# One chunk of the later modulation with each of the first five chunks of a block of w_out, in place of one with every second

## Chip, core and metric

The kernel runs on one core of one Trainium2 chip. TensorE multiplies matrices, VectorE and ScalarE (ACT) do the elementwise work, GpSimd (POOL) and SyncE (SP) issue transfers. The metric is the device time of one execution in microseconds; the number compared is the median of several executions.

## The reference

One inference step of one trunk layer over 384 tokens, 128 of context and 256 latent ones, of width 2048, all in 32-bit floats. Cut to what matters here:

```python
shift1, scale1, gate1, shift2, scale2, gate2 = split(silu(c) @ w_mod + b_mod, 6)   # c, and c_ctx for the context
h = rmsnorm(x, norm1) * (1 + scale1) + shift1
q_a, k_a, v_a, o_a, g, q_b, k_b, v_b, gate_a, gate_b = split_columns(h @ w_in)
y_a = bidirectional mLSTM of the a parts;  y_b = differential attention of the b parts
y = sigmoid(gate_a) * (y_a @ w_pa) + sigmoid(gate_b) * (y_b @ w_pb)
x = x + gate1 * (y @ w_out)
h = rmsnorm(x, norm2) * (1 + scale2) + shift2
u = depthwise convolution of width 3 over tokens of (h @ w_up)
x = x + gate2 * ((silu(u_a) * u_b) @ w_down)
result: rmsnorm(x, final_norm), and the caches and states of the context
```

`w_mod` is 2048 x 12288, that is 24 column blocks of 512; block 4 s + i belongs to the s-th of the six vectors. `shift1` and `scale1` (blocks 0 to 7) are needed before the first projection. The rest is the later modulation: gate1 (8 to 11), shift2 (12 to 15), scale2 (16 to 19), gate2 (20 to 23).

## The kernel before

All weights come from HBM in chunks of 512 KB, one `Chunk` each: SP loads it into one of six buffers (`raw`), and a chunk for a matmul is split there, in two halves (`PARTS`), into a high and a low half-precision part: ACT writes `hi` (L361), VectorE writes `lo` = raw - hi (L362); `hi` and `lo` have five buffers each. A product takes three matmuls, hi*hi, hi*lo and lo*hi: L371 to L373 where the weights are the stationary operand (`add_wstat`), L428 to L430 where the tokens are (`add_xstat`).

The order of the work is a list, `chunks`, written by hand: matmul chunks, chunks without a split, and calls (`mark`). `run()` walks it: at each place it issues the loads of up to five chunks ahead, splits up to two halves ahead, and calls `due()` before each half, which runs small work that `defer(n, f)` has put off by n halves. A scheduler below fixes the order of instructions on each engine, and gives out buffers. `settle` runs all that is still put off.

The later modulation is done on VectorE, not by matmuls. The list `by_dve` holds its 128 chunks, eight for each block, in this order: blocks 8, 16, 12; 9, 17, 13; 10, 18, 14; 11, 19, 15 (groups 0 to 3); then 20, 21, 22, 23 (group 4). Each chunk (`late_mod`, L263 and L265) has two slices of `w_mod` that are multiplied by a scalar per partition and added to an accumulator, `lacc`, once for each of two conditions: four instructions of 128 x 512. There is one buffer for the accumulator. After a block's eighth chunk, `late_sum` adds the accumulator over partitions on TensorE (L292), ACT copies the result, and either `late_out` transposes it (L301) into the modulation table, or, for the two gates, `late_row` adds the bias and writes it as a row to DRAM, by eight small transfers of POOL, from where a chunk `add_rows` reads it back over all partitions.

`spread(main, share)` mixes: it appends the chunks of `main` and, after each, as often as the running sum of `share` reaches one, the next chunk of `by_dve`. The stages in order:

- `phase_vb`, `phase_a`, `phase_gb`, `phase_ga` (parts of `w_in`, `w_pb`, `w_pa`): 16, 33, 48 and 48 chunks, shares `dens[0]` to `dens[3]`;
- four blocks of w_out, 512 columns each, `phase_out(b)`: eight matmul chunks, each 18 matmuls of 128 x 512, with the row of gate1 ahead of the last. `settle`, then the first five chunks with share `dens[4]`, then `finish_late(b)`, which puts whatever is left of groups up to b into the list, `settle`, and the other chunks. At a block's end VectorE multiplies by the gate and adds to x (L924, L926), TensorE transposes the result (L948), and ACT and VectorE scale it into the input of w_up (L953, L954, L957);
- eleven groups g of w_up, `add_up(g)`, 16 chunks each, share `dens[5]`; after g = 2 comes `finish_late(4)` and a `settle`, after g = 2, 4, 6, 8 and 10 a quarter or so of the products with w_down (`add_down`, `keep`);
- the last tokens, the norm and the outputs.

```python
for b in range(4):
    mark(settle)
    main = taken(phase_out, b)
    spread(main[:5], dens[4])
    finish_late(b)
    mark(settle)
    chunks.extend(main[5:])
...
for g in range(ngr):
    spread(taken(add_up, g), dens[5])
    if g == 2:
        finish_late(4)
        mark(settle)
```

Of the kernel before, what the change touches and what calls it, by code (L numbers as in the profile page):

```python
# [35 lines left out]
def hybrid_step(  # L36
# [1161 lines left out]
            chunks.append(by_dve.pop(0)[1])  # L1198


    dens = (.25, .25, .75, .8, .5, .5)

    def settle():
        while later:
# [130 lines left out]
```

## Time and profile before

| | |
|---|---|
| median of 3 runs | 2313.24 us |
| lowest and highest | 2309.41 and 2313.98 us |
| the profiled execution | 2311.3 us |
| its span, first to last instruction | 2309.6 us |
| mean granted clock of TensorE | 0.993 |
| read from HBM | 381.18 MB, 167 GB/s over the span |

The profile is one execution. Times in it count from the start of its span. A busy time of TensorE is that of overlapping matmuls: one of 128 x 512 lasts 0.40 us and the next starts 0.23 us after it. In a stretch row, each engine has its busy time and, in brackets, its instructions; then come the granted clock of TensorE as a share of full speed, the mean busy share of the 16 DMA engines, and GB/s. In a row of the timeline stand start and duration, engine, line, operation, operands, and in square brackets the idle time before it with what ended it. PEld is TensorE's loading of stationary operands, which runs beside the matmuls. A name before `<-` is written, those behind it are read.

### The profile page before, as it was taken

To read this page: it belongs to the slowest core of one execution; us is meant where nothing else is said; L and a number is where in the kernel's file an instruction comes from. 1 tells how busy PE (TensorE), PEld (TensorE's weight loads), DVE (VectorE), ACT (ScalarE), POOL (GpSimd) and SP (SyncE) were. 2 spreads that over 40 slices of the span, in tenths; PEclk is the share of its full clock that TensorE was granted. 3 is DMA by queue.
4 is the path that set the end of the run, shared out by engine and by line. 5 is a ranking of instruction groups with operands and counts; after the bars stand their busy time and mean duration, and the time that the engine had idled before them with its cause. 6 is when DMAs were issued, how large, how long until landed. Compare 5 with 4: busy or idle time off the path is not lost.

```text
span 2309.6 us, 34978 instructions
## 1 busy us (share of the span) xinstructions
PE 2245.2 (97%) x12814; PEld 2065.4 (89%) x12814; DVE 1637.9 (71%) x3413; ACT 1015.9 (44%) x2104; POOL 146.5 (6%) x261
## 2 busy tenths in 40 slices
PE   6999999999999999999999959999999999999998
PEld 5888997889999999987899958998899899989987
DVE  5777877777889989876789875565555555556576
ACT  5322355575555433333455522454344345434541
POOL 1000222211111100010000000000000000000000
PEclk9999999999999999999999979999999999999999
DMA  8787654445566677775656545444543543453462
GB/s 269 252 247 240 182 140 126 128 130 147 171 175 176 181 217 235 208 255 157 191 181 188 179 149 161 129 127 131 152 128 120 155 137 119 136 155 120 137 209 84
DMA packets 300300, 388.22 MB, mean 168 GB/s; under 512 B 17669, under 2 KB 215829, under 8 KB 300129
## 3 DMA queue, kind: packets, MB, share of 16 engines
q1 hardware_dynamic: 293552, 377.34, 53.6%
q0 software_dynamic: 5712, 7.09, 1.1%
q8 instruction: 100, 1.64, 0.3%
q10 hardware_dynamic: 864, 1.57, 0.2%
q14 instruction: 72, 0.58, 0.1%
HBM read 381.18 MB, written 4.76 MB: 167 GB/s over the span
## 4 chain that ended last, share of the span: by engine, by line
PE 89%; DVE 4%; DMA 3%; ACT 1%; issue 1%; POOL 0%; SPq 0%; DVEq 0%; ACTq 0%; POOLq 0%
PE mm L371 20%; PE mm L372 20%; PE mm L373 20%; PE mm L428 7%; PE mm L429 7%; PE mm L430 7%; DMA raw<-in_w_mod_dram 2%; DVE lacc L265 1%; PE mb L227 1%; DVE lo L362 1%; PE mm L1066 1%; PE mm L1065 1%; PE mm L1064 1%; PE sd L829 0%; DMA raw<-in_w_in_dram 0%
## 5 line engine op out<-in xcount | busy, mean ns | idle before, releaser
L361 ACT CAST hi<-raw 128x512 fp32r<-128x512 f32 x960 | 591.0, 620 | 1012.4 <-PE mm L372 526.4
L362 DVE TENSOR_TENSOR lo<-raw,hi 128x512 fp32r<-128x512 f32 x960 | 659.7, 693 | 482.3 <-ACT hi L361 478.3
L371 PE MATMUL mm<-hh,hi 128*128 128x386 f32 x1408 | 479.4, 340 | 0.0
L372 PE MATMUL mm<-hl,hi 128*128 128x386 f32 x1408 | 479.0, 340 | 0.0
L373 PE MATMUL mm<-hh,lo 128*128 128x386 f32 x1408 | 478.2, 340 | 0.0
L265 DVE SCALAR_TENSOR_TENSOR lacc<-raw,scT,lacc 128x512 f32<-128x512 f32 x480 | 342.0, 747 | 23.0 <-DMA raw<-in_w_mod_dram 22.8
L371 PE MATMUL mm<-xg,hi 128*128 128x384 f32 x1024 | 354.4, 347 | 2.2 <-ACT hi L361 1.4
L373 PE MATMUL mm<-xg,lo 128*128 128x384 f32 x1024 | 345.5, 337 | 0.0
L372 PE MATMUL mm<-xl,hi 128*128 128x384 f32 x1024 | 345.3, 337 | 0.0
L371 PEld LDWEIGHTS mm<-hh,hi 128*128 128x128 f32 x1408 | 267.7, 190 | 0.9 <-ACT hi L361 0.4
L372 PEld LDWEIGHTS mm<-hl,hi 128*128 128x128 f32 x1408 | 267.0, 190 | 0.2
L373 PEld LDWEIGHTS mm<-hh,lo 128*128 128x128 f32 x1408 | 266.6, 189 | 0.0
L371 PEld LDWEIGHTS mm<-xg,hi 128*128 128x128 f32 x1024 | 192.4, 188 | 21.9 <-issue 12.3
L428 PE MATMUL mm<-hi,gh 128*128 128x512 f32 x480 | 188.1, 398 | 15.3 <-ACT hi L361 14.8
L373 PEld LDWEIGHTS mm<-xg,lo 128*128 128x128 f32 x1024 | 192.2, 188 | 1.0 <-issue 0.8
L429 PE MATMUL mm<-lo,gh 128*128 128x512 f32 x480 | 190.5, 397 | 2.5 <-DVE lo L362 2.5
L372 PEld LDWEIGHTS mm<-xl,hi 128*128 128x128 f32 x1024 | 192.5, 188 | 0.5 <-issue 0.4
L430 PE MATMUL mm<-hi,gl 128*128 128x512 f32 x480 | 189.8, 395 | 0.0
L428 PEld LDWEIGHTS mm<-hi,gh 128*128 128x128 f32 x480 | 90.7, 189 | 37.1 <-ACT hi L361 15.0
L429 PEld LDWEIGHTS mm<-lo,gh 128*128 128x128 f32 x480 | 90.8, 189 | 23.8 <-DVE lo L362 3.0
L430 PEld LDWEIGHTS mm<-hi,gl 128*128 128x128 f32 x480 | 90.8, 189 | 21.5
L506 DVE TENSOR_TENSOR qk<-qk,mm 128x384 f32<-128x384 f32 x160 | 86.0, 549 | 25.0 <-PE mm L373 24.7
(333 smaller groups left out, 2974.0 us busy)
## 6 DMA issues: line engine op xcount, KB each, us to landing
raw<-in_w_mod_dram SPq DMA_DIRECT2D x192, 512.0 KB, 4.3
raw<-in_w_up_dram SPq DMA_DIRECT2D x176, 512.0 KB, 3.5
raw<-in_w_in_dram SPq DMA_DIRECT2D x160, 512.0 KB, 4.5
raw<-in_w_down_dram SPq DMA_DIRECT2D x80, 512.0 KB, 3.9
raw<-in_w_out_dram SPq DMA_DIRECT2D x32, 512.0 KB, 4.3
raw<-gate SPq DMA_DIRECT2D x28, 512.0 KB, 4.3
raw<-in_w_pb_dram SPq DMA_DIRECT2D x16, 512.0 KB, 3.8
raw<-in_w_pa_dram SPq DMA_DIRECT2D x16, 512.0 KB, 4.4
```

Of the source, the lines that this page charges most:

```text
L227: T.matmul(self.bank[32 * q:32 * q + 32, 0:self.width], lhsT=scT[:, k, 2 - 2 * i:34 - 2 * i], rhs=w[:, kk], start=i == 0 and k < 4, stop=i ...
L265: V.scalar_tensor_tensor(acc[:, j], w[:, kk], col, acc[:, j], ALU.mult, ALU.add)
L361: A.copy(h, v)
L362: V.tensor_tensor(l, v, h.bitcast(F32), ALU.subtract)
L371: T.matmul(ps, lhsT=wh, rhs=xh, start=first, stop=False)
L372: T.matmul(ps, lhsT=wh, rhs=xl, start=False, stop=False)
L373: T.matmul(ps, lhsT=wl, rhs=xh, start=False, stop=last)
L428: T.matmul(ps, lhsT=xh_[:, ts_], rhs=h[:, kk], start=k == ks[0], stop=False)
L429: T.matmul(ps, lhsT=xh_[:, ts_], rhs=l[:, kk], start=False, stop=False)
L430: T.matmul(ps, lhsT=xl_[:, ts_], rhs=h[:, kk], start=False, stop=k == ks[-1])
L506: V.tensor_tensor(dst[h][:, :NTOK], dst[h][:, :NTOK], ps, ALU.add)
L1064: T.matmul(ps, lhsT=gh[:, ts_], rhs=h, start=k == KL[0], stop=False)
```

## The change

The fifth of the six shares, used for the first five chunks of each block of w_out, goes from .5 to 1. With .5, `spread` appends a late chunk after the second and the fourth of the five; with 1, after each. Which late chunks are left for `finish_late` and for the groups of w_up follows from it; no line else is changed.

```diff
-    dens = (.25, .25, .75, .8, .5, .5)
+    dens = (.25, .25, .75, .8, 1, .5)
```

## The prediction

> **What bounds the kernel now.** I read the page's engine shares and its 40 slices first, then busy times by stretch, then the instructions in order of time where a slice falls off, and last the stage that the change loads.
>
> ```profile
> span 2309.6 us, 34978 instructions
> PE 2245.2 (97%) x12814; PEld 2065.4 (89%) x12814; DVE 1637.9 (71%) x3413; ACT 1015.9 (44%) x2104; POOL 146.5 (6%) x261
> PE   6999999999999999999999959999999999999998
> PEclk9999999999999999999999979999999999999999
> ```
>
> TensorE is busy 97% of the span, so only what leaves it idle can be won, 64.4 us in all (2309.6 - 2245.2). One slice in the middle, the 24th (each is 57.7 us, so 1328 to 1386 us), falls to 5 tenths, and there alone the granted clock falls too. The stretches around it:
>
> ```profile
> core 0: us, PE busy (x) PEld busy (x) DVE busy (x) ACT busy (x) POOL busy (x), PEclk, DMA share, GB/s
> 900.00:1000.00 100.00, 100.00 (x597) 99.07 (x596) 87.26 (x145) 37.63 (x76) 10.77 (x21) 1.00 0.77 236
> 1002.00:1037.00 35.00, 34.67 (x164) 27.47 (x163) 25.06 (x45) 11.04 (x19) 0.00 (x0) 1.00 0.68 220
> 1037.00:1073.00 36.00, 35.83 (x161) 28.64 (x160) 23.12 (x44) 13.14 (x25) 0.00 (x0) 1.00 0.52 161
> 1073.00:1109.00 36.00, 35.66 (x160) 28.43 (x159) 23.26 (x44) 12.94 (x25) 0.00 (x0) 1.00 0.55 163
> 1109.00:1144.00 35.00, 34.76 (x170) 27.43 (x169) 26.27 (x51) 14.07 (x32) 0.00 (x0) 1.00 0.60 194
> 1180.00:1352.00 172.00, 172.00 (x992) 171.11 (x991) 141.45 (x273) 82.97 (x158) 8.38 (x18) 1.00 0.58 178
> 1352.00:1386.00 34.00, 10.13 (x55) 6.90 (x54) 31.03 (x56) 7.98 (x16) 4.01 (x8) 0.60 0.50 147
> 1386.00:1500.00 114.00, 114.00 (x559) 101.82 (x558) 60.38 (x103) 40.38 (x70) 0.00 (x0) 1.00 0.47 146
> 1500.00:1700.00 200.00, 200.00 (x1038) 187.25 (x1038) 114.23 (x214) 86.14 (x159) 0.00 (x0) 1.00 0.44 135
> 1700.00:1900.00 200.00, 200.00 (x1039) 187.25 (x1038) 114.94 (x215) 86.20 (x159) 0.00 (x0) 1.00 0.44 135
> 1900.00:2100.00 200.00, 200.00 (x1039) 187.22 (x1038) 113.54 (x213) 85.45 (x157) 0.00 (x0) 1.00 0.44 136
> ```
>
> The rows at 1002, 1037, 1073 and 1109 are the four blocks of w_out, one each. From 1180 to 1352 the w_up groups g = 0 to 2 run with TensorE full; from 1386 to 2100 it is full again. Between them, in 34 us, it is busy 10.13 us, while VectorE is busy 31.03. What VectorE does there:
>
> ```profile
> 1327.89 34.02 SPq L345 DMA_DIRECT2D raw<-in_w_mod_dram  x9
> 1352.96 0.34 PE L373 MATMUL mm<-hh,lo 128*128 128x386 f32 x1
> 1353.22 0.66 PE L292 MATMUL sd<-lacc,ones 128*32 128x128 f32 x16
> 1357.46 4.72 DVE L265 SCALAR_TENSOR_TENSOR lacc<-raw,scT,lacc 128x512 f32<-128x512 f32 x7
> 1361.44 15.98 DVE L265 SCALAR_TENSOR_TENSOR lacc<-raw,scT,lacc 128x512 f32<-128x512 f32 x24
> 1364.20 5.67 SPq L345 DMA_DIRECT2D raw<-in_w_down_dram  x3
> 1367.98 1.14 ACT L361 CAST hi<-raw 128x512 fp32r<-128x512 f32 x2 [11.88 <-DMA raw<-in_w_down_dram]
> 1368.65 1.65 PE L428 MATMUL mm<-hi,gh 128*128 128x512 f32 x3 [14.76 <-ACT hi L361]
> 1376.90 1.67 PE L292 MATMUL sd<-lacc,ones 128*32 128x128 f32 x16 [6.60 <-DVE lacc L265]
> 1381.08 0.80 PE L429 MATMUL mm<-lo,gh 128*128 128x512 f32 x1 [2.50 <-DVE lo L362]
> 1381.67 0.63 PE L430 MATMUL mm<-hi,gl 128*128 128x512 f32 x1
> 1382.10 0.63 PE L429 MATMUL mm<-lo,gh 128*128 128x512 f32 x1
> 1385.51 0.42 PE L429 MATMUL mm<-lo,gh 128*128 128x512 f32 x1
> 1385.77 0.40 PE L430 MATMUL mm<-hi,gl 128*128 128x512 f32 x1
> 1386.00 0.39 PE L428 MATMUL mm<-hi,gh 128*128 128x512 f32 x1
> ```
>
> This is block 23 of the later modulation: eight chunks (`finish_late(4)` at the end of g = 2) in a row with no matmul chunk between them. SP issues their loads one behind the other, the w_down loads stand behind them in the queue and get a buffer only at 1364; VectorE works through the eight chunks from 1357 to 1377; the low halves (L362) of the first w_down chunk come behind them, and TensorE waits for ACT's high half, for the accumulator, then for the low half.
>
> **The change part by part.** First a count by the list that `spread` draws from. It holds 128 late chunks. The shares .25, .25, .75 and .8 over 16, 33, 48 and 48 matmul chunks take 4, 8, 36 and 38 of them, so 86 are gone when w_out begins. Before: two in each block of w_out and two more by `finish_late(3)` make 10; the groups g = 0 to 2 take 8 each, and 32 - 24 = 8 are left for the row above. After: five per block make 20; 22 are left; g = 0 and 1 take 8 each, g = 2 takes 6 with its second to twelfth chunk, and `finish_late(4)` finds none. So ten late chunks move into w_out, and the eight in a row are gone. Work is neither added nor removed.
>
> 1. What the eight in a row cost TensorE. The last matmul of w_up starts at 1352.96, the first one at full spacing at 1385.51: 32.55 us. Needed work in it: that last matmul (0.18), three L428 at the 0.23 us of the rows at 1385.77 and 1386.00 (0.7), the matmuls that ran between 1381.08 and 1385.51 (ten, at 0.23: 2.3) and two sums of an accumulator (L292, 0.66 each by the undisturbed one: 1.3). Together 4.5, so 28.0 us are lost. It agrees with the stretch row: 34.00 - 10.13 = 23.9 us idle, and some 4 us in which TensorE counts as busy at half pace.
>
> 2. What remains at that place. The queue of w_down chunks then follows w_up chunks directly. Of such boundaries there are three more later (after g = 4, 6 and 8), and in the rows from 1386 to 2100 TensorE is full, so I cost the boundary at nothing. Its cover is that `add_down(0)` reads products of g = 0 and 1 only, and that its loads are no longer behind eight others.
>
> 3. VectorE in w_out. A late chunk is four instructions of L265 (the first of a block has two of L263), and 24 of them took 15.98 us in the row above: 0.666 each, 2.66 us a chunk. Blocks 0, 1 and 2 get three more, 8.0 us; block 3 one more than the four it has now, 2.7 us. What VectorE has to spare in block 1:
>
> ```profile
> L362 DVE TENSOR_TENSOR lo<-raw,hi 128x512 fp32r<-128x512 f32 x17 | 11.6, 688 | 10.1 <-ACT hi L361 10.1
> L265 DVE SCALAR_TENSOR_TENSOR lacc<-raw,scT,lacc 128x512 f32<-128x512 f32 x8 | 5.7, 748 | 2.6 <-DMA raw<-in_w_mod_dram 2.6
> ```
>
> These are the groups of VectorE from 1037 to 1073. It waits 10.1 us for ACT's high halves and 2.6 for late loads, 12.7 of 36 us. Less 8.0 this leaves 4.7, so the block as a whole holds the work. Block 3 shows it nearly: it has four late chunks today, VectorE is busy 26.27 of 35, and TensorE loses 0.24 us. The stage ahead of w_out is another measure: there the share is .8, VectorE is busy 87.26 of 100 and TensorE 100.00. With 1 to 1, the splits of a chunk (two L362) and a late chunk are some 1.2 + 2.7 = 3.9 us against 18 matmuls of 0.23, 4.2 us: 93%. Tight is only the start of blocks 1 to 3, where the evacuation of the block before (three L924, three L926) and its rescaled rows (L954, L957) come on top, about 7 us. VectorE then runs behind by some 2 to 3 us and catches up in chunks six to eight, which carry no late chunk. Five buffers each of `hi` and `lo` are five half chunks of 2.1 us, so a lag of that size should not reach TensorE.
>
> 4. Loads. First the waits of VectorE from 1000 to 1160 us (total, times, longest), two short stretches with the fullest DMA engines, and the page's line on the late loads (median us to landing):
>
> ```profile
> DVE lacc L265 <- DMA raw<-in_w_mod_dram: 6.3, 6, 1.7
> DVE lacc L263 <- PE sd L292: 2.8, 2, 1.4
> 990.00:1010.00 20.00, 19.67 (x102) 17.96 (x101) 17.81 (x30) 7.70 (x15) 4.34 (x9) 1.00 0.99 353
> 1000.00:1002.00 2.00, 2.00 (x13) 2.00 (x12) 2.00 (x4) 1.15 (x2) 0.00 (x0) 1.00 1.04 387
> raw<-in_w_mod_dram SPq DMA_DIRECT2D x192, 512.0 KB, 4.3
> ```
>
> Three more loads of 512 KB in the five chunks of a block (24.5 us of its 36) are 64 GB/s over that stretch. Even on top of the fullest of these blocks' means (220) that is under the 353 to 387 GB/s that shorter stretches here reach, and block 1 with its 161 comes to about the 236 that the stage ahead carries at a full TensorE. In SP's queue the ten loads now stand between w_out loads instead of w_up and w_down loads; six buffers are shared one to one, so a w_out load gets its buffer later. VectorE runs in order. A late load lands 1.05 us after VectorE wants it (6.3 over 6 waits), at most 1.7. Behind the waiting L265 stand the low halves, and TensorE waits for those. Five waits a block of 1.05 are 5.3 us against the 4.7 spare: 0.6 us over. Bounds: with no wait nothing; with the worst, 1.7, 8.5 - 4.7 = 3.8 us a block, 15 in four. Below nothing at most the 1.1 us that TensorE idles in the four block rows now (0.33 + 0.17 + 0.34 + 0.24). I take 1.5 us for all four, near the mean wait, because in the stage at .8 TensorE loses nothing.
>
> 5. Sums that move. Block 15's sum, transposes and scale rows come in w_out's block 1 rather than 3; block 20's sum, bias row and gate row (on POOL a fill, four small loads, four small stores) in block 3 rather than in w_up, where POOL shows 0.00 busy in that row; those of 21 to 23 inside w_up. There is one accumulator, so block 21's first chunk (fourth of block 3) waits for block 20's sum on TensorE: once, 1.4 us by the row of L263 above. It is inside the 1.5.
>
> Sum against the profiled execution (2311.3 us, span 2309.6): 2311.3 - 28.0 + 1.5 = 2284.8. That execution lies 1.9 us under the median of the three runs (2313.24), inside their spread of 4.6, so I forecast 2285 us.
>
> One rule weighed against a row: the stretch with the stall has a granted clock of 0.60 where its neighbours have 1.00, and matmuls come every 0.43 us (1381.67, 1382.10) for 4.4 us after the stall, which costs 2.1 us of the 28.0. The Trainium skill, in "TensorE: Matmul & The Clock Gate", section "What's actually happening", says that an idle window of about 3.4 us halves the clock and as long a busy one restores it. By that figure the slow tail would cost an estimated 1.7 us and the sum would be 2285.2; by the row it is 2.1 and 2284.8. The trace agrees with the mechanism, and its length is somewhat longer.
>
> **The rivals.** (a) w_out gives half of it back. The late loads come 1.7 us late each, VectorE overruns by 3.8 us a block and the low halves with it: 15 us, 2298. For it: six buffers shared by ten loads instead of seven in five chunks' time. Against it: the .8 stage. The same section of the Trainium skill implies that a gap of over 3.4 us would also leave TensorE at half clock for a while; no block of w_out idles over 0.34 us in all today.
>
> (b) It ends slower. Same place, but each late load is issued only when VectorE frees a buffer, so that its flight is wholly exposed: 5 x 4.3 - 4.7 = 16.8 us a block, 67 in four, 2350. It decides from a mean wait of (7.0 + 4.7) / 5 = 2.3 us per late load on, where four blocks lose 28. Against it: no wait over 1.7 in 1000 to 1160.
>
> (c) The boundary at 1352 keeps a stall of its own: the last w_up evacuation and the first w_down splits come together on VectorE, the way TensorE waited 2.50 for L362 and 6.60 for the sum. 9 us, 2294. Against it: the later boundaries.
>
> (d) The change does not do what it says: the scheduler keeps late instructions at the end of g = 2 whatever their place in the list, and nothing moves, 2311. Against it: in the rows the loads and L265 stand where the list has them.
>
> **How the numbers follow.** Forecast 0.74; (a) 0.13; (b) 0.03; (c) 0.06; (d) 0.04. Three runs of one kernel spread over 4.6 us (0.2%), about what a measurement tells from no change. The low end is 2311.3 - 28.0 - 1.1 with the spread's lower arm of 1.9: 2280. The high end takes in (c) and nearly all of (a): 2297. Faster: forecast, (a) and (c), 0.93; within 0.2%: most of (d), 0.04; slower: (b), 0.03.
>
> **What would show it.** Right: no slice in the middle under 9; no group of L265 longer than four or five at the end of g = 2; TensorE full from 1150 to the end phase; clock 1.00 there; VectorE at some 30 of 35 us in each w_out block; TensorE's idle time in w_out between 1 and 4 us in all. Wrong: TensorE idle by over 3 us in a w_out block before L429 (low half late) or L428 (high half late), with VectorE waiting for raw<-in_w_mod more than 1.7 us a time; or an idle stretch left where w_down begins.

## The result and the profile after

The changed kernel takes 2289.23 us, the median of four runs (2288.35 to 2291.11), against 2312.91 before (2309.41 to 2313.98): a ratio of 0.9901 with an interval from 0.9884 to 0.9918. It is 1.0% faster, 23.7 us; 2285 with a range of 2280 to 2297 was forecast. The profiled execution took 2289.29 us.

First the page after: span, engines, and the slices of TensorE and its clock.

```profile
span 2287.6 us, 34989 instructions
PE 2242.5 (98%) x12814; PEld 2064.0 (90%) x12814; DVE 1636.5 (72%) x3413; ACT 1014.9 (44%) x2104; POOL 146.5 (6%) x261
PE   6999999999999999999999999999999999999998
PEclk9999999999999999999999999999999999999999
```

The slice with a 5 is gone, in TensorE and in its clock. TensorE's idle time is 45.1 us (2287.6 - 2242.5) where it was 64.4. The stretches after, with the columns of those before; the first four are w_out:

```profile
1002.00:1037.00 35.00, 33.13 (x156) 26.49 (x157) 30.68 (x54) 10.84 (x19) 0.00 (x0) 1.00 0.70 225
1037.00:1073.00 36.00, 34.73 (x170) 27.45 (x170) 31.88 (x60) 13.48 (x29) 0.00 (x0) 1.00 0.69 227
1073.00:1109.00 36.00, 35.26 (x158) 28.17 (x157) 28.14 (x52) 12.83 (x25) 0.00 (x0) 1.00 0.63 199
1109.00:1144.00 35.00, 32.16 (x151) 25.29 (x150) 24.44 (x48) 11.30 (x22) 2.26 (x5) 0.95 0.49 154
1180.00:1330.00 150.00, 150.00 (x868) 149.10 (x868) 129.93 (x250) 74.54 (x142) 6.18 (x13) 1.00 0.60 187
1330.00:1386.00 56.00, 56.00 (x294) 50.61 (x293) 32.88 (x64) 24.36 (x45) 2.00 (x4) 1.00 0.44 133
```

From 1330 to 1386, over the boundary between w_up and w_down, TensorE is now full. In w_out it is not: 6.7 us idle in these four rows (1.87, 1.27, 0.74, 2.84) against 1.1 before, and the clock of the fourth is 0.95.

Where the 22.0 us between the two spans lie can be read from four marks in the timelines. Before, the first matmul of w_up and the last of TensorE (the last of w_up before the boundary started at 1352.96, shown above):

```profile
1144.15 0.34 PE L371 MATMUL mm<-hh,hi 128*128 128x386 f32 x1
2299.04 0.27 PE L1066 MATMUL mm<-rl,gl 128*128 128x128 f32 x1
```

After, the same two, and between them the last of w_up and the first of w_down, with the w_down loads of SP that now come well ahead:

```profile
1150.50 0.33 PE L371 MATMUL mm<-hh,hi 128*128 128x386 f32 x1
1328.74 8.62 SPq L345 DMA_DIRECT2D raw<-in_w_down_dram  x3
1359.68 0.34 PE L373 MATMUL mm<-hh,lo 128*128 128x386 f32 x1
1359.85 0.40 PE L428 MATMUL mm<-hi,gh 128*128 128x512 f32 x1
2277.02 0.27 PE L1066 MATMUL mm<-rl,gl 128*128 128x128 f32 x1
```

| stretch | before | after | difference |
|---|---|---|---|
| to the first matmul of w_up | 1144.15 | 1150.50 | +6.35 |
| w_up, g = 0 to 2 | 208.81 | 209.18 | +0.37 |
| from there to TensorE's end | 946.08 | 917.34 | -28.74 |
| sum | 2299.04 | 2277.02 | -22.02 |

The row of eight was worth 28.7 us, and w_out gave 6.4 of it back.

Where w_out loses them: the waits from 990 to 1160 us of TensorE, and from 1000 to 1160 of VectorE and ScalarE (total, times, longest). The first line is that of before, the others are of after:

```profile
PE sd L948 <- DVE x1t L926: 0.7, 3, 0.3
PE sd L948 <- DVE x1t L926: 4.9, 3, 2.8
PE mm L428 <- DVE sig L894: 2.1, 1, 2.1
DVE lacc L265 <- DMA raw<-in_w_mod_dram: 8.2, 6, 2.2
ACT hi L361 <- DMA raw<-in_w_out_dram: 14.6, 5, 4.5
```

Between these two profiles the 2.1 at L894 is no loss: TensorE came there earlier than before and left at 1003.87, as it had (1003.89). In the kernels below this wait lies between 0 and 3.2 us, with the old order in w_out and with the new one; how much of it belongs to the change is open. The three waits at L948 are the three borders between blocks. The longest, in order of time:

```profile
1096.79 1.41 DVE L265 SCALAR_TENSOR_TENSOR lacc<-raw,scT,lacc 128x512 f32<-128x512 f32 x2 [1.75 <-DMA raw<-in_w_mod_dram]
1102.79 2.08 DVE L265 SCALAR_TENSOR_TENSOR lacc<-raw,scT,lacc 128x512 f32<-128x512 f32 x3 [1.46 <-DMA raw<-in_w_mod_dram]
1108.34 0.75 DVE L265 SCALAR_TENSOR_TENSOR lacc<-raw,scT,lacc 128x512 f32<-128x512 f32 x1 [2.20 <-DMA raw<-in_w_mod_dram]
1112.80 1.29 DVE L924 TENSOR_TENSOR mm<-mm,raw 128x512 f32<-128x512 f32 x2
1114.00 1.27 DVE L926 TENSOR_TENSOR x1t<-x1t,mm 128x512 f32<-128x512 f32 x2
1114.82 0.46 PE L948 MATMUL sd<-cst,x1t 128*128 128x128 f32 x2 [2.84 <-DVE x1t L926]
1116.36 0.63 PE L430 MATMUL mm<-hi,yl 128*128 128x512 f32 x1
1116.79 0.63 PE L428 MATMUL mm<-hi,yh 128*128 128x512 f32 x1
1115.00:1118.50 3.50, 3.50 (x12) 2.80 (x11) 2.07 (x4) 0.20 (x1) 0.00 (x0) 0.51 0.91 307
```

VectorE waits three times for a late chunk of the next block, 5.4 us between 1095.0 and 1108.3. The evacuation of the finished block (L924, L926) stands behind these in its order and starts at 1112.80; before, it started at 1107.82, and TensorE stood 0.24 us at this border. TensorE has the transposes of that result (L948) next and stands 2.84 us; then it runs at half clock (0.51) until 1118.5, with a matmul every 0.43 us. The three waits, 4.2 us more than before, and an estimated 1.6 us for the half clock (seven matmuls at 0.23 us and four short transposes in the 3.66 us from 1114.82 on) make up 5.8 of the 6.4.

### The profile page after: what moved, and what is told of

Its sections match the earlier page's. It is cut to its first block, busy times and chain, and to the rows that moved or that the text cites. A ratio compares the mean times of both kernels' runs of the same rounds, so it can differ in the third digit from the quotient of the medians.

```text
span 2287.6 us, 34989 instructions
## 1 busy us (share of the span) xinstructions
PE 2242.5 (98%) x12814; PEld 2064.0 (90%) x12814; DVE 1636.5 (72%) x3413; ACT 1014.9 (44%) x2104; POOL 146.5 (6%) x261
## 4 chain that ended last, share of the span: by engine, by line
PE 86%; DVE 6%; DMA 5%; issue 1%; ACT 1%; POOL 0%; SPq 0%; DVEq 0%; ACTq 0%; POOLq 0%
PE mm L371 20%; PE mm L372 19%; PE mm L373 19%; PE mm L428 7%; PE mm L429 7%; PE mm L430 7%; DMA raw<-in_w_mod_dram 2%; DVE lacc L265 2%; DVE lo L362 2%; PE mb L227 1%; DMA raw<-in_w_in_dram 1%; DMA raw<-in_w_down_dram 1%; DMA raw<-in_w_out_dram 1%; PE mm L1066 1%; PE mm L1065 1%
## 5 line engine op out<-in xcount | busy, mean ns | idle before, releaser
L361 ACT CAST hi<-raw 128x512 fp32r<-128x512 f32 x960 | 590.9, 620 | 1003.3 <-PE mm L372 528.4
L265 DVE SCALAR_TENSOR_TENSOR lacc<-raw,scT,lacc 128x512 f32<-128x512 f32 x480 | 342.9, 748 | 22.9 <-DMA raw<-in_w_mod_dram 22.6
L429 PE MATMUL mm<-lo,gh 128*128 128x512 f32 x480 | 189.3, 394 | 0.0
L430 PEld LDWEIGHTS mm<-hi,gl 128*128 128x128 f32 x480 | 90.1, 188 | 21.3
L429 PEld LDWEIGHTS mm<-lo,gh 128*128 128x128 f32 x480 | 90.1, 188 | 20.7
```

The lines of the kernel that those rows point to most:

```text
L265: V.scalar_tensor_tensor(acc[:, j], w[:, kk], col, acc[:, j], ALU.mult, ALU.add)
L361: A.copy(h, v)
L429: T.matmul(ps, lhsT=xh_[:, ts_], rhs=l[:, kk], start=False, stop=False)
L430: T.matmul(ps, lhsT=xl_[:, ts_], rhs=h[:, kk], start=False, stop=k == ks[-1])
```

## The experiments

Two questions: is the row of eight by itself the 28.7 us, and what in w_out costs the 6.4. For the second there were three theories: A, the place of the late chunks ahead of the evacuation; B, too much work on VectorE; C, late loads that land late.

**The row taken away without touching w_out.** The kernel before, with all 32 chunks of group 4 spread over w_up:

```diff
-        spread(taken(add_up, g), dens[5])
+        spread(taken(add_up, g), (0.69, 0.69, 0.63)[min(g, 2)])
```

> The kernel before with its .5 in w_out, and shares of .69, .69 and .63 in the first three groups of w_up, so that these take all 32 chunks of group 4 and none is left for the end of g = 2. Theory: the eight in a row cost 28 to 29 us by themselves (before against after, from the last matmul of w_up to the last one of TensorE: 946.1 against 917.3), and VectorE has room in w_up (141.45 of 172 us busy, eight more chunks are 21.3). So 2311.3 - 28.7 = 2282.6, w_out as before with 1.1 us of idle time, w_up 209 us long as before. Rival: VectorE is too full in w_up at 163 of 172 us, evacuations come late there as they do in w_out of the changed kernel, at a price of 1 us a group or more than 2 us in all: 2286 or more.

Measured: 2283.19 us against 2311.99 in the same session, ratio 0.9882 (0.9867 to 0.9896): 28.8 us. Its stretches of w_up and of the boundary:

```profile
1150.00:1330.00 180.00, 180.00 (x1051) 178.47 (x1050) 168.31 (x335) 92.09 (x177) 10.43 (x22) 1.00 0.63 196
1330.00:1400.00 70.00, 70.00 (x345) 60.47 (x344) 48.90 (x87) 27.73 (x50) 2.00 (x4) 1.00 0.56 177
```

VectorE is busy 168.31 of 180 in w_up and TensorE 180.00. The row is the gain, and w_out is not needed for it.

**The row kept, w_out changed.** The changed kernel with eight left over:

```diff
-        spread(taken(add_up, g), dens[5])
+        spread(taken(add_up, g), (0.3126, 0.3126, 0.25)[min(g, 2)])
```

> The changed kernel with 1 in w_out, but with shares of .3126, .3126 and .25 in the first three groups of w_up, so that eight chunks are left in a row at the end of g = 2 again. Theory: the two parts add up. The row costs its 28.7 us again, w_out its 6.4 us: 2311.3 + 6.4 = 2317.7, slower than before by 0.3%. Rival: what w_out lost in the profile after was a chance of that execution or was hidden anyway: 2311 to 2313, as before.

Measured: 2317.2, ratio 1.0022 (1.0012 to 1.0031), 5.2 us slower. The row is back, as one group of VectorE and a stretch of TensorE (1365 and 1359 on this kernel's clock):

```profile
1365.02 19.96 DVE L265 SCALAR_TENSOR_TENSOR lacc<-raw,scT,lacc 128x512 f32<-128x512 f32 x30
1359.00:1394.00 35.00, 11.13 (x60) 7.84 (x59) 31.03 (x56) 7.98 (x16) 4.00 (x8) 0.61 0.49 147
```

The two parts add up: +5.2 for w_out alone and -28.8 for the row alone make -23.6, and the change gave -23.7.

**Same work in w_out, two chunks later.** Late chunks behind the third to seventh matmul chunk of a block:

```diff
-        spread(main[:5], dens[4])
+        chunks.extend(main[:2])
+        spread(main[2:7], dens[4])
...
-        chunks.extend(main[5:])
+        chunks.extend(main[7:])
```

> The changed kernel with the five late chunks of a block behind the third to seventh matmul chunk in place of the first to fifth. Same loads and same work in each block. Theory A (place): w_out loses its 6.4 us at the borders of its blocks alone, where the late chunks of the next block, loaded ahead, stand before the evacuation (L924, L926) on VectorE; two chunks later they stand behind it, the transposes (L948) don't wait, and w_out is back at 1 to 2 us of idle time: 2284 to 2285. Rival B (amount): VectorE has too much to do in a block, wherever it stands: 2289 as after, with the idle time elsewhere in the block.

Measured: 2281.61, ratio 0.9871 (0.9857 to 0.9886). Waits of TensorE and VectorE in w_out:

```profile
PE sd L948 <- DVE x1t L926: 0.5, 1, 0.5
DVE lacc L265 <- DMA raw<-in_w_mod_dram: 2.9, 3, 1.3
```

It is 2.4 us under what A expected. The borders cost 0.5 us in place of 4.9. B falls: the work is the same. But VectorE's waits for loads fell too, so A and C are not told apart by this.

**A seventh load buffer.** The place as in the change:

```diff
-    rawp = ctx.enter_context(tc.tile_pool(name="rawp", bufs=6))
+    rawp = ctx.enter_context(tc.tile_pool(name="rawp", bufs=7))
...
-        LD, SPL = 5, 2
+        LD, SPL = 6, 2
...
-NSLOT = 50
+NSLOT = 49
...
-            sel = sp.tile([P, P], R32, name=nm("sel"), tag="sel", bufs=4)
+            sel = sp.tile([P, P], R32, name=nm("sel"), tag="sel", bufs=2)
```

> The changed kernel with seven load buffers and loads issued six chunks ahead (for the room: 49 in place of 50 of the 128 x 388 buffers, and two in place of four of the row selectors of the mLSTM). Theory C (late loads): VectorE stands still 8.2 us for late loads between 1000 and 1160, and that makes the evacuation late; a buffer more brings each load about one chunk (2 us) earlier, VectorE waits under 3 us and w_out loses 1 to 3 us in place of 6.4: 2284 to 2286, if the other stages stay as they are. Rival B (amount of work on VectorE): the waits go and the stalls stay, 2289.

Measured: 2276.53 (2276.02 to 2277.10), ratio 0.9849 (0.9834 to 0.9864), the fastest of all. Waits as above and the stretch that holds w_out:

```profile
PE sd L948 <- DVE x1t L926: 0.8, 2, 0.5
DVE lacc L265 <- DMA raw<-in_w_mod_dram: 3.8, 4, 1.3
1000.00:1150.00 150.00, 149.23 (x715) 120.35 (x713) 128.39 (x233) 59.22 (x124) 4.21 (x9) 1.00 0.67 219
```

VectorE is busier in this stretch than in the change (128.39 us against 121.79) and TensorE idles 0.8 us. VectorE's waits for late chunks halved to 3.8 us, where under 3 was expected. So with the place of the change a buffer alone cures it, and A as the sole cause falls. The time is 7.5 us under the low end of what was expected; the rest of the gain lies outside w_out (two runs below).

**Small loads.** The late chunks in w_out load 64 columns, which the four instructions read eight times over:

```diff
-            S.dma_start(out=self.v, in_=self.src)
+            if self.lite:
+                S.dma_start(out=self.v[:, :, 0:64], in_=self.src[:, :, 0:64])
+            else:
+                S.dma_start(out=self.v, in_=self.src)
...
```

> The changed kernel, but the 20 late chunks in w_out load 64 of their 512 columns (64 KB in place of 512), and their four instructions on VectorE read these columns eight times over: as many elements, an eighth of the transfer. It leaves out seven eighths of these columns of the modulation. Place, order in the list and buffers as after. Theory C (late landing): the loads land earlier, VectorE's waits for them in 1000 to 1160 fall from 8.2 to under 3 us, and TensorE's idle time in w_out from 7 to 1 to 3 us: 2282 to 2285. Rival A (place alone): the late work stands before the evacuation whether its data are there or not; waits go, stalls stay: 2288 to 2289.

Measured: 2281.61, ratio 0.9873 (0.9858 to 0.9887). The waits of VectorE and ScalarE from 1000 to 1160 (L269 and L368 in this kernel are L265 and L361 in the others), and the stretch:

```profile
DVE lacc L269 <- DMA raw<-in_w_mod_dram: 3.5, 6, 1.0
ACT hi L368 <- DMA raw<-in_w_out_dram: 11.9, 5, 3.1
1000.00:1150.00 150.00, 150.00 (x722) 121.44 (x721) 128.71 (x235) 60.54 (x127) 4.22 (x9) 1.00 0.53 160
```

TensorE is busy 150.00 of 150, with VectorE as busy as with seven buffers. VectorE still waits six times for a late chunk, 3.5 us where under 3 was expected, but 1.0 us at most in place of 2.2. With late loads of an eighth of the size w_out loses nothing, though place and work are those of the change, so C holds, and A, the place alone, falls. The w_out loads share the queue, and in the change they are late too: ScalarE waits 14.6 us for them, where before it had no such wait. Here it still waits 11.9 us, and TensorE stands nowhere. That points to the late chunks rather than to the w_out loads; how the 6.4 us divide between them was not separated, since the longest wait for a w_out load fell too, from 4.5 to 3.1 us.

**A quarter of the work.** The same 20 chunks with full loads and one instruction in place of four:

```diff
-        for kk in range(2):
-            for j in range(2):
+        for kk in range(1 if lite else 2):
+            for j in range(1 if lite and kg else 2):
...
```

> The changed kernel, but the 20 late chunks in w_out have one instruction of L265 in place of four (two of L263 at a block's first chunk), with full loads. It leaves out three quarters of their sums. Theory C: a load still has to land, and what VectorE waits for it is spent in its queue before the evacuation; but a buffer is given back 2 us earlier, so about half of the stall stays: 2284 to 2287, with waits for raw<-in_w_mod of 3 to 8 us. Rival B (amount of work): VectorE has 10 x 2 = 20 x 2.0 = 40 us less to do in w_out, no stalls: 2281 to 2283.

Measured: 2287.29, ratio 0.9897 (0.9883 to 0.9912).

```profile
PE sd L948 <- DVE x1t L926: 3.7, 3, 2.4
DVE lacc L265 <- DMA raw<-in_w_mod_dram: 20.7, 12, 3.0
1000.00:1150.00 150.00, 144.35 (x676) 115.45 (x675) 86.31 (x162) 51.21 (x99) 4.21 (x9) 0.99 0.66 214
```

VectorE is idle for 64 us of 150 and the evacuation is late all the same. It waits 20.7 us for late loads where 3 to 8 were expected; with less to do it stands earlier at the next one. B is refuted a second time; the price is the landing.

**Seven buffers without the change.** Once without a row, once with it:

> Seven load buffers (as in the run with seven buffers) with .5 in w_out and all of group 4 in w_up. If what the seventh buffer wins outside w_out (about 4 us behind the last boundary of w_up and w_down) adds to the version without a row of eight at 2283: 2277 to 2279. If its gain lay in w_out alone: 2283.

Measured: 2279.08, ratio 0.9860 (0.9846 to 0.9875), 4.1 us under the same version with six buffers (2283.19, run in another session).

> Seven load buffers in the kernel before, .5 in w_out, eight chunks in a row at the end of g = 2. Theory: the row is VectorE work (20 us) and stays; a seventh buffer lets one w_down load in behind the row sooner, which spares at most the 2 to 3 us of the wait for the high half, and about 4 us elsewhere: 2305 to 2309. Rival: the row costs its time because the w_down loads stand behind the eight in SP's queue; then a buffer more should win 5 us or more at that place: under 2303.

Measured: 2306.55, ratio 0.9978 (0.9968 to 0.9987), 4.8 us under before. Waits of TensorE around the row, 1345 to 1390:

```profile
PE mm L428 <- ACT hi L361: 12.2, 1, 12.2
PE sd L292 <- DVE lacc L265: 9.2, 1, 9.2
PE mm L429 <- DVE lo L362: 2.5, 1, 2.5
```

23.9 us, and with six buffers 23.9 as well (14.76 + 6.60 + 2.50). A w_down load came in earlier, and TensorE waited for the accumulator instead: the row is bounded by VectorE, not by its loads' place in SP's queue. The seventh buffer's 4 to 5 us are thus neither there nor, mostly, in w_out. The traces place most of them later: from the last matmul of w_up ahead of the first w_down chunk to the last one of all w_up it takes 842.98 us before and 839.43 with a seventh buffer, 814.40 and 811.16 without a row, 813.62 and 810.35 with the change. That is 3.2 to 3.6 us, though from 1400 to 2220 TensorE shows as busy for 817.9 to 820.0 of 820 us in all six; why its matmuls come closer together was not taken apart.

**Sixteen and four in a row**, both in the kernel before, by other shares in w_up.

> The kernel before with .5 in w_out and shares of .375, .3126 and .3126 in the first three groups of w_up: sixteen late chunks are left in a row at the end of g = 2 in place of eight. Theory (the row is work of VectorE, 2.66 us a chunk, and a fixed rest of 7.4 us for the hand-over and the half clock): eight more cost 21.3 us: 2333. Rival (loads bound the row: each of the chunks of 512 KB comes at 2.65 us or slower because six buffers turn over once per landing of 4.3 us plus 2.66 of work): the same or up to 2.2 us a chunk more, if VectorE is seen waiting for them: 2333 to 2350.

Measured: 2332.86 against 2310.40, ratio 1.0097 (1.0082 to 1.0112): 22.5 us for eight more, 2.8 a chunk. VectorE shows two groups:

```profile
1362.87 19.96 DVE L265 SCALAR_TENSOR_TENSOR lacc<-raw,scT,lacc 128x512 f32<-128x512 f32 x30
1384.86 19.96 DVE L265 SCALAR_TENSOR_TENSOR lacc<-raw,scT,lacc 128x512 f32<-128x512 f32 x30
```

No wait for a load lies in either: thirty instructions in 19.96 us, 0.665 each. The row is VectorE's work.

> The kernel before with .5 in w_out and shares of .63, .57 and .57 in the first three groups of w_up: four late chunks left in a row. Theory (2.66 us a chunk and a fixed rest of 7.4): 28.7 - 10.6 = 18.1 us lost, 2300.7. Rival (part of a short row is hidden, since matmuls already split ahead run beside it: five half chunks of hi and lo are 10 us): under 10 us lost, 2286 to 2292.

Measured: 2296.39, ratio 0.9940 (0.9924 to 0.9957), 14.0 us under before. Against the 28.8 of eight, four cost 14.8: neither the 18.1 of the straight line nor the under 10 of the rival.

```profile
1354.10 0.86 PE L428 MATMUL mm<-hi,gh 128*128 128x512 f32 x3
1364.30 1.67 PE L292 MATMUL sd<-lacc,ones 128*32 128x128 f32 x16 [9.34 <-DVE lacc L265]
1366.41 0.79 PE L429 MATMUL mm<-lo,gh 128*128 128x512 f32 x1 [0.44 <-DVE lo L362]
```

The w_down load is there before the row ends, so the wait for ACT's high half (14.76 with eight) is gone and the only long one is for the accumulator, 9.34. A constant rest beside 2.66 a chunk was too simple for a short row.

**Both cures in one**: seven buffers and the later place.

> Seven load buffers, and the late chunks of w_out behind the third to seventh matmul chunk, share 1. Each alone gave 2276.5 and 2281.6 us. Theory: both cure the same waits of w_out, so little adds there (w_out idles 0.8 us with seven buffers): 2275.5 to 2277. Rival: they are separate gains and add, 2276.5 - 7.6 = 2269.

Measured: 2278.23, ratio 0.9859 (0.9845 to 0.9874). They do not add; it is 1.7 us above seven buffers alone, a little outside what was expected.

## Why the prediction was right, step by step

The direction, the range and the mechanism of the gain held; 23.7 us came of the 28.0 that step 1 allowed. The forecast of 2285 lies 4.2 us below the measured time, and the range holds it because its high end made room for rival (a). The loss in w_out came by another path than the one forecast.

- The count of late chunks: right. Nothing is left at the end of g = 2.
- Step 1, the price of the row: 28.0 predicted, 28.74 between the marks of the two traces, 28.8 when it was taken away alone. Also its reason: eight more cost about what eight times VectorE's four instructions take.
- Step 2, the boundary costs nothing without the row: right, 56.00 of 56 and 70.00 of 70. Rival (c) did not come.
- Step 3, VectorE's room in w_out: right as to the amount. With 128 us of work in 150 TensorE is full, once the loads land in time. Its last sentence is wrong: it set a lag of VectorE against the buffers of `hi` and `lo` alone, and the lag reached TensorE by the evacuation.
- Step 4 is the term that was mis-sized: 1.5 us for w_out, 6.35 measured. It took 1.05 us a wait from the row of before and let five such waits a block just overrun VectorE's spare time. Six waits came in all of w_out, fewer than the twenty allowed for. But their mean was 1.37 (8.2 over 6) and the longest 2.2, and they were not spread over a block: three came in the last 18 us before an evacuation. The spare time of a whole block does not help there. The place of the harm was wrong too: TensorE has no wait for a low half (L429) in w_out; it waited at the transposes (L948) for the evacuation, ahead of which nothing can be stored. The 24.5 us that the step gives to five of a block's eight chunks have no row behind them; five eighths of 36 us are 22.5, which makes 70 GB/s in place of 64 and changes no term.
- Rival (a) named the cause (late loads, six buffers shared one to one) with 15 us; it came with two fifths of that, and not by the low halves. Its note that a gap would also halve the clock came true once, behind 2.84 us, a shorter gap than the note names.
- Step 5: right, block 21's wait for the accumulator is not seen to hold TensorE.
- Of the signs, those for w_up and the boundary came. TensorE's idle time in the four rows of w_out was 6.7 us and not 1 to 4, and VectorE's waits of over 1.7 us, a sign of being wrong, came with 2.2; but TensorE stood under 3 us in each row, and before L948.

## What to carry to other kernels

Work of a second engine that is put off to a deadline cost nothing here while it was spread over w_up, and 28.8 us for eight chunks in a row at a stage's end, more than their 21.3 us of work: look in the timeline for a long group of one line beside an idle bounding engine. Before it is moved into an earlier stage, ask not only whether that engine has room on average but what its instruction order puts behind a load that may be late: an evacuation at the border of a block has no stock to live on. A load buffer more, or two chunks' distance from the border, did there what less work did not.

## What the hardware showed that had not been expected

TensorE's clock halved after shorter gaps than rival (a) names, and not every time. After 2.84 us idle it was 0.51 (the row from 1115); in the kernel with a quarter of the work it was 0.54 after 2.45 us at one border, and stayed 1.00 after 2.48 us where w_out begins:

```profile
1080.82 0.48 PE L948 MATMUL sd<-cst,x1t 128*128 128x128 f32 x2 [2.45 <-DVE x1t L926]
1080.80:1084.50 3.70, 3.68 (x12) 2.96 (x13) 2.87 (x5) 0.17 (x1) 0.00 (x0) 0.54 0.71 212
1007.05 0.50 PE L428 MATMUL mm<-hi,yh 128*128 128x512 f32 x1 [2.48 <-DVE sig L894]
1007.00:1010.00 3.00, 2.94 (x13) 2.44 (x14) 3.00 (x6) 1.80 (x4) 0.00 (x0) 1.00 0.92 316
```

The Trainium skill, in "TensorE: Matmul & The Clock Gate", section "What's actually happening", says that an idle window of about 3.4 us halves the clock, and that the window runs freely and does not start with the work. These rows differ from the first figure: a gap a microsecond shorter was enough. That equal gaps had different outcomes fits a window that is not tied to them; why 2.4 us can be enough no run here shows.
